# Quarter products of two SwiGLU layers start in another order

## Chip, core and metric

One NeuronCore of a Trainium2 chip runs the whole program. The metric is the device time of one execution in microseconds (us). The kernel before has a median of 958.43 us over three runs (958.37, 958.43 and 960.74). One other execution was profiled, and all rows shown here come from it.

## What is computed

A streaming-encoder block on `x` of shape (1, 512, 1024), all in float32. Cut to the parts that matter here:

```python
h = h + 0.5 * _swiglu(_rmsnorm(h, ffn1_norm[i]), ffn1_w_in[i], ffn1_w_out[i])   # first layer
z = _rmsnorm(h, mix_norm[i]) @ w_in[i]          # convolution module and gated linear attention
h = h + concat([y_conv, y_gla]) @ w_out[i]
h = h + 0.5 * _swiglu(_rmsnorm(h, ffn2_norm[i]), ffn2_w_in[i], ffn2_w_out[i])   # second layer
gate = sigmoid(_rmsnorm(h, ple_norm[i]) @ ple_w_gate[i])
h = h + gate * (p[i] @ ple_w_proj[i])           # then a last rmsnorm

def _swiglu(x, w_in, w_out):
    gate, up = split(x @ w_in, 2)
    return (silu(gate) * up) @ w_out
```

Each of the two SwiGLU layers has 1024 inputs, 2816 gate and 2816 up columns, and 512 tokens. They are the two "layers" of this text.

## The kernel before, in words

**Three products for one.** Every float32 operand is split into a high part (rounded to float32r) and a low part (what is left), and each product is three matmuls: high x high, high x low, low x high. ScalarE (ACT) casts the high part of a weight (`wh`), VectorE (DVE) subtracts to get the low part (`wl`); this is `part` (L406). In the other way, `add_part` (L412, through `added`, L198), ACT writes the negated weight into `wl`, and a DMA that GpSimd (POOL) issues adds the weight to it, so that DVE has no work.

**Seven products for eight.** The 2816 gate columns go in 11 pairs of 128-column blocks, numbered 0 to 10. A pair's weight has four quarters: `a11`, `a12` for the gate (rows 0 to 511 and 512 to 1023 of the input), `a21`, `a22` for up. The tokens are two halves. A pair is done as 2x2 blocks in the manner of Strassen and Winograd, with seven products of 24 matmuls each (128x256), named m1 to m7: m1 uses `a11`, m2 `a12`, m4 `a22`; m6, m7, m5 and m3 use the weight sums `s2`, `s3`, `s1`, `s4` that DVE makes (`s12`, `s3_`, `s4_`, L417 to L434). On the other side stand `b` quarters and their sums `t1` to `t4` (class `Right`, L329), which ACT and DVE split as well (`split`, L360). Below, m1(2) is product m1 of pair 2.

**Banks.** m1 opens the PSUM bank `p.x`; ACT copies it to `p.a` (`sq` in the profile). m6 adds to the same bank; ACT copies that to `p.u2` (`u` in the profile), and m5, which adds to the bank once more, has to wait for that copy (L673 to L683). m2 has its own bank `p.y`. m7 opens `p.w`; DVE reads it in m5's `plus` (`u<-ps,sq`), and m4, which adds to `p.w`, has to wait for that (L681 to L687).

**The gates.** After m2, `gate0` (L668) adds m1's copy to m2's bank and multiplies by the row scale on DVE (two instructions, `g`), and ACT takes silu of it (`s`). It was put behind the next product's preparations.

**The order.** `ffn` (L604) lists *units*, a product each, and `drive` (L584) writes them out: ahead of each product come the preparations that are due for later ones, `AHEAD` = 4 units early for a split on DVE, 6 units for `add_part`, 7 and 9 for a fetch, 6 for sums. The engines run their instructions strictly in that order. In the first layer pair 1 runs as a plain product without sums (units h0 to h7, 128x512) while the token sums are prepared; then pairs 2 to 10 follow. In the second layer pair 1 is the first in quarters. Between the products stand pieces of the second matmul (`w_out`, `wo` below), two 12-matmul groups of 128x512 at a time. Weights come by DMAs that SyncE (SP) issues, into six raw buffers (`wr`); an issue waits until its buffer is free.

The starting order is written out by hand: m1(start), m2(start), m1(start+1), and then for each pair m6, m7, m5, the next pair's m2, m4, m3 (L826 to L844). Pair 2 of the first layer is the first in quarters, so start = 2 there, and start = 1 in the second.

Of the kernel before, what the change touches and what calls it, by code (L numbers as in the profile page):

```python
# [62 lines left out]
def block_kernel(ctx: ExitStack, tc: tile.TileContext, a: dict, out: bass.AP):  # L63
# [29 lines left out]
    def tmp(s, w=SEQ, dt=F32, bufs=2):  # L93
        return tp.tile([P, w], dt, tag=s, bufs=bufs, name=nm(s))

    def bank():
        return pp.tile([P, SEQ], F32, tag="mm", bufs=7, name=nm("ps"))

    def aux():
        return pp.tile([P, SEQ], F32, tag="aux", bufs=1, name=nm("ax"))  # L100
# [113 lines left out]
    def ahead(src, c0, ncol):  # L214


        return [[added(w) for w in high4(load(src, 0, DC, c, P))] for c in range(c0, c0 + ncol, P)]
# [41 lines left out]
    def spread(col, copy=True):  # L259

        ps = aux()
        for j in range(TB):
            pe.transpose(ps[:, j * P:(j + 1) * P], col[:, j:j + 1].to_broadcast([P, P]), ident)
        if not copy:
            return ps
        bc = tmp("bc", bufs=1)
        act.copy(bc, ps)
        return bc
# [17 lines left out]
    class Norm:  # L286
# [5 lines left out]
        def add(self, h):  # L292
            if self.n == 0:
                act.activation(self.acc, h, AF.Square)
            else:
                sq = tmp("sq", bufs=3)
                act.activation(sq, h, AF.Square)
                self.engine.tensor_tensor(out=self.acc, in0=self.acc, in1=sq, op=ALU.add)
            self.n += 1
# [8 lines left out]
    def mul(ps, w, x, first, last, ks=range(4)):  # L308

        (wh, wl), k0 = w, ks[0]  # L310
        for k in ks:
            xh, xl = x[k]
            for i in range(2):
                cs = slice(i * P, (i + 1) * P)
                o = ps[:, i * HALF:(i + 1) * HALF]
                end = last and k == ks[-1] and i == 1
                pe.matmul(o, wh[:, k - k0, cs], xh, start=(first and k == ks[0] and i == 0), stop=False, skip_group_check=True)
                pe.matmul(o, wh[:, k - k0, cs], xl, start=False, stop=False, skip_group_check=True)
                pe.matmul(o, wl[:, k - k0, cs], xh, start=False, stop=end, skip_group_check=True)
# [117 lines left out]
    ffn1_in = a["ffn1_w_in"][0]  # L437
    hT = [big.tile([P, SEQ], F32, tag="H", bufs=DC, name=nm("h")) for _ in range(DC)]
    hg, xps, xt, squares = [], [], {}, []
# [74 lines left out]
    w1 = Left(ffn1_in, 2)  # L514
# [9 lines left out]
    ps0 = [bank() for _ in range(4)]  # L524
    split_w(0, 1, dve.tensor_copy)
    split_x(0)
    mid = []
# [22 lines left out]
    xb = Right(hg, "ffn1_norm")  # L550
    steps = xb.steps()
# [49 lines left out]
        for f in left:  # L601
            f()

    def ffn(w_in, w_out, x, gname, given, first, rsb, hooks, plain, adds=()):  # L604


        norm = Norm()
        nhg = []
        got = {}
        npair = DFF // (2 * P)  # L610
        start = 1 + len(plain)
        end = npair - 1
        pairs = {i: given.get(i) or Left(w_in, 2 * i) for i in range(npair)}

# [8 lines left out]
        def silu(g):  # L623
            s = tmp("s")
            act.activation(s, g, AF.Silu)
            return s

        def plus(ps, t, i, name):
            o = tmp(name)
            dve.tensor_tensor(out=o, in0=ps, in1=t, op=ALU.add)  # L630
            dve.tensor_tensor(out=two(o), in0=two(o), in1=row(i), op=ALU.mult)
            return o
# [11 lines left out]
        def snap(ps, name, **kw):  # L644
            o = tmp(name, **kw)
            act.copy(o, ps)
            return o
# [16 lines left out]
        def m2(p):  # L664
            p.y = bank()
            mul(p.y, p.part("a12"), x.op["b21"], True, True)

            def gate0():  # L668
                p.s0 = silu(plus(p.y, p.a, 0, "g1"))

            return [gate0]

        def m6(p):  # L673
            mul(p.x, p.part("s2"), x.op["t2"], False, False)
            p.u2 = snap(p.x, "u2", bufs=1)

        def m7(p):
            p.w = bank()
            mul(p.w, p.part("s3"), x.op["t3"], True, False)
# [14 lines left out]
        def plain_unit(j):  # L694

            up, i, k = j // 4, j // 2 % 2, j % 2
            def run(p):
# [17 lines left out]
            return run  # L715

        USES = {"m1": ("a11", m1), "m2": ("a12", m2), "m6": ("s2", m6), "m7": ("s3", m7), "m5": ("s1", m5),
                "m4": ("a22", m4), "m3": ("s4", m3)}

        def unit(kind, i):  # L720
            p = pairs[i]

            def go(run):
                left = run(p)
                hooks.get((kind, i), lambda *_: None)()
                return left

            if kind[0] == "h":
                j = int(kind[1])
                part, run = (f"a{1 + j // 4}{1 + j % 2}", plain_unit(j)) if j % 4 < 2 else (None, plain_unit(j))  # L730
                if part:
                    make = p.add_part if (kind, i) in adds else p.part
                    return [(AHEAD, lambda: make(part)), (9, lambda: p.fetch(part))], lambda: go(run)
            else:
                part, run = USES[kind]
            if (kind, i) in adds:
                before = [(AHEAD + 2, lambda: p.add_part(part))]
            else:
                before = [(AHEAD + (kind == 'm5'), lambda: p.part(part))] if part else []
            if kind in ("m1", "m2"):  # L740
                before.append((7, lambda: p.fetch(part)))
            elif kind == "m6":
                before += [(9, lambda: p.fetch("a21", "a22")), (6, p.s12)]
            elif kind in ("m7", "m3"):
                before.append((6, p.s3_ if kind == "m7" else p.s4_))

            return before, lambda: go(run)
# [63 lines left out]
        def add(kind, i):  # L811
            if 0 <= i < npair and (kind, i) not in had:
                had.add((kind, i))
                units.append(unit(kind, i))
# [3 lines left out]
        for i in plain:  # L818
# [4 lines left out]
                    due = due[1:]  # L823
            if i in cut_of:
                due += second(cut_of[i])
        add("m1", start)  # L826
        add("m2", start)
        add("m1", start + 1)
        for i in range(start, npair):
            add("m6", i)  # L830
            add("m7", i)
# [34 lines left out]
    w_in = a["w_in"][0]  # L866
    w_ahead = []

    def sums_hooks(x, names, at):

        h = {}
        for name, key in zip(names, at):
            h[key] = lambda *_, name=name: x.split(name)
        return h

    hooks = sums_hooks(xb, ("t2", "t3", "t1", "t4"), (("h2", 1), ("h3", 1), ("h4", 1), ("m1", 2)))
    hooks.update({("h0", 1): lambda *_: [f() for f in steps[2:4]], ("h1", 1): steps[4]})
    hooks.update({("m5", 3): lambda *_: made[0](), ("m5", 4): lambda *_: constants(),
                  ("m4", 10): lambda *_: w_ahead.append(ahead(w_in, D_CONV, 2 * P)),
                  ("last", 4): lambda *_: w_ahead.append(ahead(w_in, 0, 2 * P))})  # L880
    hg, norm = ffn(ffn1_in, a["ffn1_w_out"][0], xb, "mix_norm", {0: Left(ffn1_in, 0), 1: w1},
                   (ps0[:2], ps0[2:]), lambda: spread(mid[0]), hooks, (1,),
                   {("h4", 1), ("m1", 2), ("m2", 2), ("m4", 2)})
    pool.on = False
    cw, gwu, mean, mask, nbias = made

# [61 lines left out]
    mid = []  # L948
# [10 lines left out]
    rs, rsb = mid  # L959
# [16 lines left out]
    for k0 in range(0, DC, 4):  # L976
        for i in range(2):
            for j in range(4):
                pe.matmul(ps[2 * RANK * j:2 * RANK * (j + 1)], gw[:, k0 + j, :], hg[k0 + j][i].bitcast(F32),
                          start=(k0 == i == 0), stop=(k0 + i == 5), skip_group_check=True)  # L980
# [337 lines left out]
    ffn2_in = a["ffn2_w_in"][0]  # L1318
    wf = {i: Left(ffn2_in, 2 * i) for i in range(3)}
    w0, w1 = wf[0], wf[1]  # L1320
# [40 lines left out]
    norm = Norm()  # L1361
# [57 lines left out]
    hg = nhg  # L1419

    def plain_block(p, up, i, mid={}):
        ps = bank()
        cs = slice(i * P, (i + 1) * P)
        for k in range(DC):
            if k in mid:
                mid[k]()
            wh, wl = p.part(f"a{1 + up}{1 + k // 4}")
            mm3(ps, wh[:, k % 4, cs], wl[:, k % 4, cs], *hg[k], k == 0, k == DC - 1)
        return ps

    mid = []
    xb = Right(hg, "ffn2_norm")
    steps = xb.steps()
# [4 lines left out]
    g0 = plain_block(w0, 0, 0)  # L1438
    steps[1]()
    steps[2]()  # L1440
    u0 = plain_block(w0, 1, 0, {4: lambda: mid.append(norm.rows())})
# [4 lines left out]
    g1_ = plain_block(w0, 0, 1, {1: lambda: mid.append(spread(mid[0]))})  # L1446
# [5 lines left out]
    u1_ = plain_block(w0, 1, 1)  # L1452
    xb.split("t1")
    w1.part("s3")
    hooks = sums_hooks(xb, ("t4",), (("m2", 1),))
# [63 lines left out]
    def todo(*fs):  # L1519
        return lambda *_: [f(*v) for f, *v in fs]  # L1520
# [4 lines left out]
                  ("rest", 2): todo((q_high, b21, q21, 0), (first_sum, 0), (third_sum, 0)),  # L1525
                  ("rest", 4): todo((q_high, b21, q21, 1), (first_sum, 1), (third_sum, 1)),
                  ("rest", 6): todo((final_in,), (row_sums, 0))})
    hg, norm = ffn(ffn2_in, a["ffn2_w_out"][0], xb, "ple_norm", wf, ((g0, u0), (g1_, u1_)), mid[1], hooks, ())

# [143 lines left out]
    def kept(ps, name, **kw):  # L1675
        o = tmp(name, **kw)
        act.copy(o, ps)
        return o
# [20 lines left out]
    t1, t3 = q11, q12  # L1699
    n2_ = [x for jp in range(2) for x in split_rows(n2, jp)]  # L1700
    project(0)
    m1 = [kept(p_, "sq", bufs=3) for p_ in x_]
# [98 lines left out]
```

## Time and profile before

| | us |
|---|---|
| Median of three runs | 958.43 |
| Profiled execution, its own time | 958.56 |
| Its span in the profile | 956.8 |
| TensorE (PE) busy | 936.5 (98%) |
| DVE busy | 762.8 (80%) |
| ACT busy | 484.9 (51%) |

The profile's rows read: start, duration, engine, line, operation, output <- inputs, and in brackets the idle time before it and what ended that. Nearly all instructions have line 46, a recorder's, so that they are told apart by their tiles.

### The profile page before, as it was taken

What the parts mean: (1) busy time and instruction counts of PE and PEld (TensorE: products, weight loads), DVE (VectorE), ACT (ScalarE), POOL (GpSimd) and SP (SyncE); (2) the same over time, 40 slices, a digit from 0 to 9 for tenths busy, and PEclk for the clock granted to TensorE, in tenths of its full rate; (3) what the DMA queues carried; (4) which work ended last, traced back from release to release, by engine and by line L of the source; (5) the groups of instructions that cost most, each with busy time, mean ns of one, the idle gap of its engine ahead of it and who ended that gap; (6) DMA issues with size and microseconds to landing.
All of it is one profiled execution on the core that took longest, in us unless ns stands there. A gap on an engine that the chain in (4) does not pass through costs nothing.

```text
span 956.8 us, 14725 instructions
## 1 busy us (share of the span) xinstructions
PE 936.5 (98%) x5914; PEld 835.7 (87%) x5914; DVE 762.8 (80%) x1037; ACT 484.9 (51%) x729; POOL 57.7 (6%) x75
## 2 busy tenths in 40 slices
PE   9997999999999999999999999999999999999996
PEld 7887999999999988788877889999999999998885
DVE  5787778877878666999987689887887787875896
ACT  5863434344444463374564775444334443445882
POOL 0100010000000020101020010000000000000131
PEclk9998999999999999999999999999999999999999
DMA  7644233423243395337454563323343224347463
GB/s 227 178 111 132 80 100 108 125 79 106 89 132 94 94 245 144 89 66 199 94 117 121 133 133 109 111 84 104 100 132 90 88 88 133 95 133 231 94 110 110
DMA packets 108264, 115.01 MB, mean 120 GB/s; under 512 B 5203, under 2 KB 96517, under 8 KB 108196
## 3 DMA queue, kind: packets, MB, share of 16 engines
q1 hardware_dynamic: 101732, 94.67, 32.1%
q0 software_dynamic: 6448, 19.40, 11.2%
q8 instruction: 46, 0.75, 0.3%
q14 instruction: 22, 0.18, 0.1%
q10 hardware_dynamic: 16, 0.00, 0.0%
HBM read 93.61 MB, written 2.10 MB: 100 GB/s over the span
## 4 chain that ended last, share of the span: by engine, by line
PE 92%; DVE 4%; ACT 3%; issue 1%; POOLq 0%; POOL 0%; ACTq 0%; DVEq 0%
PE ps L46 90%; PE ax L46 1%; ACT wh L46 1%; DVE wl L46 1%; DVE g L46 1%; ACT xg L46 1%; ACT s L46 0%; ACT wl L46 0%; DVE m L46 0%; ACT sq L46 0%; DVE sm L46 0%; DVE xg L46 0%; DVE t1L L46 0%; DVE u L46 0%; DVE wr L46 0%
## 5 line engine op out<-in xcount | busy, mean ns | idle before, releaser
L46 PE MATMUL ps<-hgH,wl 128*128 128x256 f32 (+1 forms) x768 | 230.9, 306 | 2.0 <-DVE wl L46 1.9
L46 PE MATMUL ps<-hgH,wh 128*128 128x256 f32 (+1 forms) x768 | 232.5, 308 | 0.0
L46 PE MATMUL ps<-hgL,wh 128*128 128x256 f32 (+1 forms) x768 | 230.9, 306 | 0.0
L46 DVE TENSOR_TENSOR wl<-wr,wh 128x1024 fp32r<-128x1024 f32 (+2 forms) x160 | 187.5, 1182 | 47.5 <-ACT wh L46 47.4
L46 ACT CAST wh<-wr 128x1024 fp32r<-128x1024 f32 (+2 forms) x178 | 179.3, 1021 | 18.7 <-issue 6.7
L46 PEld LDWEIGHTS ps<-hgH,wl 128*128 128x128 f32 x768 | 146.8, 191 | 9.2 <-DVE wl L46 2.5
L46 PEld LDWEIGHTS ps<-hgH,wh 128*128 128x128 f32 x768 | 147.1, 192 | 8.6 <-issue 1.1
L46 PEld LDWEIGHTS ps<-hgL,wh 128*128 128x128 f32 x768 | 146.4, 191 | 6.8 <-issue 0.2
L46 PE MATMUL ps<-actH,wh 128*128 128x512 f32 x352 | 137.5, 391 | 0.0
L46 PE MATMUL ps<-actL,wh 128*128 128x512 f32 x352 | 137.4, 390 | 0.0
L46 PE MATMUL ps<-actH,wl 128*128 128x512 f32 x352 | 136.9, 389 | 0.0
L46 ACT ACTIVATE s<-g 128x512 f32<-128x512 f32 x48 | 30.4, 634 | 200.6 <-DVE g L46 200.6
L46 DVE SCALAR_TENSOR_TENSOR cv<-glu,cw,cv 128x502 f32<-128x502 f32 (+24 forms) x120 | 81.1, 733 | 0.6
L46 PEld LDWEIGHTS ps<-actH,wl 128*128 128x128 f32 x352 | 66.1, 188 | 14.0
L46 PEld LDWEIGHTS ps<-actH,wh 128*128 128x128 f32 x352 | 66.2, 188 | 12.8
L46 PEld LDWEIGHTS ps<-actL,wh 128*128 128x128 f32 x352 | 66.2, 188 | 12.4
L46 DVE SCALAR_TENSOR_TENSOR h<-ps,h 128x512 f32<-128x512 f32 x80 | 54.2, 687 | 19.2 <-PE ps L46 19.2
L46 ACT COPY sq<-ps 128x512 f32<-128x512 f32 x42 | 24.5, 585 | 78.7 <-PE ps L46 78.7
L46 DVE TENSOR_TENSOR wl<-sm,wh 128x1024 fp32r<-128x1024 f32 x42 | 51.0, 1222 | 3.3 <-ACT wh L46 3.1
L46 PE MATMUL ps<-t1H,wh 128*128 128x256 f32 x152 | 44.4, 292 | 8.0 <-ACT u L46 8.0
L46 ACT CAST wh<-sm 128x1024 fp32r<-128x1024 f32 x42 | 43.9, 1046 | 6.0 <-DVE sm L46 3.3
L46 PE MATMUL ps<-t1L,wh 128*128 128x256 f32 x152 | 44.1, 290 | 0.0
(267 smaller groups left out, 1774.6 us busy)
## 6 DMA issues: line engine op xcount, KB each, us to landing
wr<-in_ffn_w_in SPq DMA_DIRECT2D x84, 512.0 KB
wr<-in_ffn_w_out SPq DMA_DIRECT2D x32, 512.0 KB
wr<-in_w_in SPq DMA_DIRECT2D x20, 512.0 KB
wl<-wr POOLq DMA_DIRECT2D x19, 512.0 KB, 5.1
wr<-in_ffn_w_out SPq DMA_DIRECT2D x16, 384.0 KB
wr<-in_w_out SPq DMA_DIRECT2D x8, 512.0 KB
wq<-in_ple_w_gate SPq DMA_DIRECT2D x8, 512.0 KB
wl<-wq POOLq DMA_DIRECT2D x8, 512.0 KB, 4.9
```

What stands on the lines that cost most here:

```text
L46: inst = call(*args, **kwargs)
```

## The change

It does three things.

1. Both layers get a number `lead`. The gate of the pair `start + lead - 1` isn't left behind the next product; it is held and written out in m6 of pair `start`, right behind the copy of u2. In the first layer `lead` is 2, so that this is the gate of pair 3; in the second it is 1, the gate of pair 1.
2. In the first layer the plain products of two pairs come first: m1(2), m2(2), m1(3), m2(3), and then m6(2). m2(3) moves from behind m5(2) to ahead of m6(2).
3. In the first layer the weight sums of pair 2 are made in h3 and h4, with the splits of `t3` and `t1`, and the set of products whose low parts are added by DMA changes: m1(2) leaves it (DVE subtracts again), m1(3) and m2(3) join it.

```diff
-    def ffn(w_in, w_out, x, gname, given, first, rsb, hooks, plain, adds=()):
+    def ffn(w_in, w_out, x, gname, given, first, rsb, hooks, plain, lead, adds=()):
...
+        held = []
...
                 p.s0 = silu(plus(p.y, p.a, 0, "g1"))
+            if p is pairs[start + lead - 1]:
+                held.append(gate0)
+                return []
             return [gate0]
         def m6(p):
             mul(p.x, p.part("s2"), x.op["t2"], False, False)
             p.u2 = snap(p.x, "u2", bufs=1)
+            for f in held:
+                f()
+            held.clear()
...
-        add("m1", start)
-        add("m2", start)
-        add("m1", start + 1)
+        for i in range(start, start + lead):
+            add("m1", i)
+            add("m2", i)
+        if lead == 1:
+            add("m1", start + 1)
...
+    wf = {i: Left(ffn1_in, 2 * i) for i in (2,)}
+    hooks.update({("h0", 1): lambda *_: [f() for f in steps[2:4]], ("h1", 1): steps[4],
+                  ("h3", 1): lambda *_: [xb.split("t3"), wf[2].s12()], ("h4", 1): lambda *_: [xb.split("t1"), wf[2].s3_()]})
...
-                   {("h4", 1), ("m1", 2), ("m2", 2), ("m4", 2)})
+                   (ps0[:2], ps0[2:]), lambda: spread(mid[0]), hooks, (1,), 2,
+                   {("h4", 1), ("m2", 2), ("m4", 2), ("m1", 3), ("m2", 3)})
...
-    hg, norm = ffn(ffn2_in, a["ffn2_w_out"][0], xb, "ple_norm", wf, ((g0, u0), (g1_, u1_)), mid[1], hooks, ())
+    hg, norm = ffn(ffn2_in, a["ffn2_w_out"][0], xb, "ple_norm", wf, ((g0, u0), (g1_, u1_)), mid[1], hooks, (), 1)
```

**First place: ACT ahead of m1(2), first layer.** Before, where `wr_495` is `a11` of pair 2, `wr_520` its `a12`, and `s` the silu of plain gates:

```order
L46 CAST wh_497<-wr_429 128x1024
L46 CAST wh_522<-wr_495 128x1024
L46 ACTIVATE wl_523<-wr_495 128x1024
L46 ACTIVATE s_529<-g_117_527 128x512
L46 CAST t2H_544<-xg_422 128x512
L46 CAST t2H_548<-xg_491 128x512
L46 CAST wh_554<-wr_520 128x1024
L46 ACTIVATE wl_555<-wr_520 128x1024
L46 CAST t3H_571<-xg_416 128x512
L46 CAST t3H_575<-xg_482 128x512
L46 ACTIVATE s_581<-g_131_579 128x512
```

And now, where `wr_495` is still `a11` of pair 2, `wr_516` its `a12`, and `wr_547` is `a11` of pair 3:

```order
L46 CAST wh_497<-wr_429 128x1024
L46 ACTIVATE s_520<-g_113_518 128x512
L46 CAST t2H_535<-xg_422 128x512
L46 CAST t2H_539<-xg_491 128x512
L46 CAST wh_549<-wr_516 128x1024
L46 ACTIVATE wl_550<-wr_516 128x1024
L46 CAST t3H_566<-xg_416 128x512
L46 CAST t3H_570<-xg_482 128x512
L46 CAST wh_580<-wr_547 128x1024
L46 ACTIVATE wl_581<-wr_547 128x1024
L46 CAST wh_585<-wr_495 128x1024
L46 ACTIVATE s_591<-g_136_589 128x512
```

The cast of `a11` of pair 2, which the first product in quarters needs, has moved from the second place to the eleventh, behind both a silu and two other weights.

**Second place: DVE between the first weights of pair 3 and m4(2), first layer.** Before, where `sm_844` is the first weight sum of pair 3 (`wr_741` is its `a21`, `wr_743` its `a22`) and `u_181` is the instruction that m4(2) waits for:

```order
L46 TENSOR_TENSOR sm_844<-wr_741,wr_743 128x1024
L46 TENSOR_TENSOR sm_845<-sm_844,wr_552 128x1024
L46 TENSOR_TENSOR wl_849<-wr_520,wh_848 128x1024
L46 TENSOR_TENSOR u_181_878<-ps_819,sq_876 128x512
L46 TENSOR_TENSOR u_181_878<-u_181_878,bc_454 128x512
L46 TENSOR_TENSOR wr_741<-wr_552,wr_741 128x1024
L46 TENSOR_TENSOR wl_883<-wr_786,wh_882 128x1024
```

And now, where these are `sm_850`, `wr_746`, `wr_748` and `u_186`:

```order
L46 TENSOR_TENSOR sm_850<-wr_746,wr_748 128x1024
L46 TENSOR_TENSOR sm_851<-sm_850,wr_547 128x1024
L46 TENSOR_TENSOR wl_855<-wr_516,wh_854 128x1024
L46 TENSOR_TENSOR wr_746<-wr_547,wr_746 128x1024
L46 TENSOR_TENSOR wl_885<-wr_787,wh_884 128x1024
L46 TENSOR_TENSOR u_186_914<-ps_858,sq_912 128x512
L46 TENSOR_TENSOR u_186_914<-u_186_914,bc_454 128x512
```

Two more 1024-wide subtractions now stand ahead of the instruction that m4(2) waits for.

**Third place: DVE where the second layer's gate is held.** Before, where `g_984` is the gate of pair 1, `sm_5711` the first sum of pair 2, and `u_998` is what m4(1) waits for:

```order
L46 TENSOR_TENSOR g_984_5679<-ps_5641,sq_5631 128x512
L46 TENSOR_TENSOR g_984_5679<-g_984_5679,bc_5491 128x512
L46 TENSOR_TENSOR sm_5711<-wr_5598,wr_5600 128x1024
L46 TENSOR_TENSOR sm_5712<-sm_5711,wr_5373 128x1024
L46 TENSOR_TENSOR wr_5598<-wr_5373,wr_5598 128x1024
L46 TENSOR_TENSOR wl_5743<-wr_5034,wh_5742 128x1024
L46 TENSOR_TENSOR wl_5774<-sm_5712,wh_5773 128x1024
L46 TENSOR_TENSOR u_998_5803<-ps_5746,sq_5801 128x512
```

And now:

```order
L46 TENSOR_TENSOR sm_5707<-wr_5599,wr_5601 128x1024
L46 TENSOR_TENSOR sm_5708<-sm_5707,wr_5374 128x1024
L46 TENSOR_TENSOR g_989_5737<-ps_5642,sq_5632 128x512
L46 TENSOR_TENSOR g_989_5737<-g_989_5737,bc_5492 128x512
L46 TENSOR_TENSOR wr_5599<-wr_5374,wr_5599 128x1024
L46 TENSOR_TENSOR wl_5744<-wr_5035,wh_5743 128x1024
L46 TENSOR_TENSOR wl_5775<-sm_5708,wh_5774 128x1024
L46 TENSOR_TENSOR u_998_5804<-ps_5747,sq_5802 128x512
```

The gate's two instructions have moved behind the two sums; the count ahead of `u_998` is the same. On ACT the silu of that gate has moved from ahead of the copies `sq` and `u` to behind them, and still stands ahead of the cast that `wl_5744` needs:

```order
L46 CAST wh_5676<-wr_5376 128x1024
L46 COPY sq_5705<-ps_5680 128x512
L46 COPY u_988_5735<-ps_5607 128x512
L46 ACTIVATE s_5740<-g_989_5737 128x512
L46 CAST wh_5743<-wr_5035 128x1024
L46 CAST wh_5774<-sm_5708 128x1024
```

More of the change, by code (lines that the diff above doesn't have):

```diff
@@ L876, in block_kernel @@
     hooks = sums_hooks(xb, ("t2", "t3", "t1", "t4"), (("h2", 1), ("h3", 1), ("h4", 1), ("m1", 2)))
-    hooks.update({("h0", 1): lambda *_: [f() for f in steps[2:4]], ("h1", 1): steps[4]})
+    wf = {i: Left(ffn1_in, 2 * i) for i in (2,)}
+    hooks.update({("h0", 1): lambda *_: [f() for f in steps[2:4]], ("h1", 1): steps[4],
+                  ("h3", 1): lambda *_: [xb.split("t3"), wf[2].s12()], ("h4", 1): lambda *_: [xb.split("t1"), wf[2].s3_()]})
     hooks.update({("m5", 3): lambda *_: made[0](), ("m5", 4): lambda *_: constants(),
@@ L880, in block_kernel @@
                   ("last", 4): lambda *_: w_ahead.append(ahead(w_in, 0, 2 * P))})
-    hg, norm = ffn(ffn1_in, a["ffn1_w_out"][0], xb, "mix_norm", {0: Left(ffn1_in, 0), 1: w1},
-                   (ps0[:2], ps0[2:]), lambda: spread(mid[0]), hooks, (1,),
-                   {("h4", 1), ("m1", 2), ("m2", 2), ("m4", 2)})
+    hg, norm = ffn(ffn1_in, a["ffn1_w_out"][0], xb, "mix_norm", {0: Left(ffn1_in, 0), 1: w1, 2: wf[2]},
+                   (ps0[:2], ps0[2:]), lambda: spread(mid[0]), hooks, (1,), 2,
+                   {("h4", 1), ("m2", 2), ("m4", 2), ("m1", 3), ("m2", 3)})
     pool.on = False
```

## The prediction

> **What bounds the kernel now.** I read the page's chain first: TensorE has nearly all of it.
>
> ```profile
> PE 92%; DVE 4%; ACT 3%; issue 1%; POOLq 0%; POOL 0%; ACTq 0%; DVEq 0%
> ```
>
> So only what stops PE counts. The waits of PE (total, times, longest) name two that the change can touch:
>
> ```profile
> PE ps L46 <- ACT u L46: 8.0, 2, 6.1
> PE ps L46 <- DVE wl L46: 1.9, 2, 1.7
> ```
>
> The wait for `u` is m5's for the copy of u2, once in each layer. PE's timeline shows the long one, in the first layer:
>
> ```profile
> 65.88 0.28 PE L46 MATMUL ps<-t2H,wh 128*128 128x256 f32 x1
> 68.76 0.28 PE L46 MATMUL ps<-t3H,wh 128*128 128x256 f32 x1
> 71.52 0.28 PE L46 MATMUL ps<-t3H,wl 128*128 128x256 f32 x1
> 77.86 0.58 PE L46 MATMUL ps<-t1H,wh 128*128 128x256 f32 x1 [6.06 <-ACT u L46]
> 83.15 0.31 PE L46 MATMUL ps<-hgH,wh 128*128 128x256 f32 x1
> 86.06 0.40 PE L46 MATMUL ps<-actH,wh 128*128 128x512 f32 x1
> 91.52 0.28 PE L46 MATMUL ps<-hgH,wh 128*128 128x256 f32 x1
> ```
>
> m6(2) begins at 65.88 and m7(2) at 68.76: a product costs 2.88 us. m5(2) begins 6.2 us late, at 77.86, and takes 5.29 us instead of 2.88. m2(3) follows, then two `wo` groups of 5.46 us together, and m4(2) at 91.52. The windows tell why m5 is slow (the columns after DVE's are ACT's, POOL's, the granted clock, the DMA share and GB/s):
>
> ```profile
> 71.80:77.80 6.00, 0.00 (x1) 0.00 (x0) 4.10 (x5) 3.38 (x6) 0.86 (x1) 0.88 0.47 90
> 77.80:83.20 5.40, 5.34 (x25) 5.34 (x26) 3.70 (x4) 0.96 (x2) 0.00 (x0) 0.50 0.62 192
> ```
>
> The clock was at 0.50 after the stop: 2.41 us more. The stop costs 8.6 us in all, and there is 1.7 us ahead of it and 1.9 us in the second layer. That is the most that can go, some 12 us.
>
> **The change, first layer, step by step.** I add durations along each engine's queue in the new order, on the clock of this profile. Up to 49 us nothing differs. ACT before:
>
> ```profile
> 44.85 2.00 ACT L46 CAST wh<-wr 128x1024 fp32r<-128x1024 f32 x2
> 49.90 0.63 ACT L46 ACTIVATE s<-g 128x512 f32<-128x512 f32 x1 [2.10 <-DVE g L46]
> 52.43 1.06 ACT L46 ACTIVATE wl<-wr 128x1024 fp32r<-128x1024 f32 x1
> 53.38 1.13 ACT L46 CAST t3H<-xg 128x512 fp32r<-128x512 f32 x2
> ```
>
> A 1024-wide cast takes 0.95 us from start to start, a 512-wide one 0.52. The second of the casts at 44.85 is `a11` of pair 2. Now that cast stands behind the silu at 49.90, which still waits for DVE, and behind two more weights. ACT reaches it after the `t3` casts, at 53.38 + 1.04 + 1.90 = 56.3, and ends it at 57.4. Its low part is DVE's:
>
> ```profile
> 55.05 0.28 PE L46 MATMUL ps<-hgH,wh 128*128 128x256 f32 x1
> 54.03 1.30 DVE L46 TENSOR_TENSOR t3L<-xg,t3H 128x512 fp32r<-128x512 f32 x2 [1.65 <-ACT t3H L46]
> 58.34 1.22 DVE L46 TENSOR_TENSOR sm<-wr,wr 128x1024 f32<-128x1024 f32 x1
> 59.60 1.23 DVE L46 TENSOR_TENSOR sm<-sm,wr 128x1024 f32<-128x1024 f32 x1
> 64.34 2.36 DVE L46 TENSOR_TENSOR wl<-sm,wh 128x1024 fp32r<-128x1024 f32 x2
> ```
>
> After the `t3` splits DVE makes the two sums (1.26 + 1.14) and then this `wl`, which ends at 58.9. m1(2) could begin at 55.05; its third matmul, due at 55.29, now comes at 58.97. **A new stop of 3.7 us** takes the place of the 1.7 us one at m1(3), whose low part now comes by DMA. That gate of DVE is late too, so ACT's silu runs at 59.6, and `a12` of pair 3 leaves ACT at 63.2. How long the DMA takes after POOL's issue:
>
> ```profile
> 47.18 0.37 SPq L176 DMA_DIRECT2D wr<-in_ffn_w_in  x1
> 48.11 0.86 POOL L46 DMA_DIRECT2D wl<-wr  x1 [10.80 <-ACT wl L46]
> wl<-wr POOLq DMA_DIRECT2D x1, 512.0 KB, 6.1
> 53.78 0.86 POOL L46 DMA_DIRECT2D wl<-wr  x1 [4.80 <-ACT wl L46]
> wl<-wr POOLq DMA_DIRECT2D x1, 512.0 KB, 4.5
> ```
>
> The one issued at 48.11, beside a load of SP, landed after 6.1 us; the one at 53.78, alone, after 4.5. The new one is issued at 63.5, within 0.2 us of a `w_out` load that goes when the third sum has freed its buffer (63.2). I take 6.1: it lands at 69.6, and m2(3) stops 2.0 us (4.5 would stop it 0.45). PE's list is then m1(2) to 61.6, m2(2) 64.5, m1(3) 67.4, m2(3) 72.2, m6(2) 75.1, m7(2) 78.0.
>
> Is u2 copied in time? On ACT two subtractions' worth of casts for m5 and m7, `a22`, the silu of gate 2, a copy and a `wo` cast lie ahead; DVE's gate ends at 73.1 and the copy begins when m6 has ended, about 75.2. **So m5's stop goes**, and with it the half clock: m5(2) ends at 80.9, the two `wo` groups at 86.3.
>
> **Then m4(2) waits, which it didn't before.** It needs DVE's `u<-ps,sq`, which has two more subtractions ahead. The head of that queue is the first sum of pair 3, and what it waits for is a chain of transfers:
>
> ```profile
> 72.02 0.86 POOL L46 DMA_DIRECT2D wl<-wr  x1 [17.38 <-ACT wl L46]
> 76.62 0.37 SPq L176 DMA_DIRECT2D wr<-in_ffn_w_in  x1
> 80.25 1.23 DVE L46 TENSOR_TENSOR sm<-wr,wr 128x1024 f32<-128x1024 f32 x1 [1.67 <-DMA wr<-in_ffn_w_in]
> 84.00 0.69 DVE L46 TENSOR_TENSOR u<-ps,sq 128x512 f32<-128x512 f32 x1
> ```
>
> `a22` of pair 2 is added by DMA (72.02 to 76.6); that frees a raw buffer, and SP loads `a22` of pair 3 into it (76.62 to 80.2). In the new order ACT hands `a22` over at 71.5, behind the casts for m5 and m7, and POOL issues at 71.8. SP's load of `a21` for pair 3, which was issued at 67.86 before, now goes at 71.9, when m7's `wl` has freed its buffer. So the two run together: 71.8 + 6.1 = 77.9, the load 3.6 more, 81.5. Then 1.26 + 4 x 1.14 for two sums, s4's low part, the third sum and a `wo` low part: 87.3, and 0.7 for `u`. m4(2) begins at 88.05 instead of 91.52. From there on both lists are alike and m2(3) lies behind both, so **the first layer gains 3.5 us**. PE's own new stops (3.7 and 2.0) cost nothing more: without them m4(2) would only wait longer. If POOL's DMA takes 4.5 there, m4(2) begins at 86.5: 5.0 us. DVE comes out of this some 4 us behind PE; the next stop would be m4(3), two thirds of a pair later, and DVE has idle time there (2.45 us ahead of `u`):
>
> ```profile
> 112.19 0.69 DVE L46 TENSOR_TENSOR u<-ps,sq 128x512 f32<-128x512 f32 x1 [2.45 <-ACT sq L46]
> ```
>
> **The change, second layer.**
>
> ```profile
> 586.11 0.38 PE L46 MATMUL ps<-t1H,wh 128*128 128x256 f32 x1 [1.90 <-ACT u L46]
> 584.47 0.63 ACT L46 ACTIVATE s<-g 128x512 f32<-128x512 f32 x1 [3.79 <-DVE g L46]
> 585.47 0.59 ACT L46 COPY u<-ps 128x512 f32<-128x512 f32 x1
> 582.97 0.68 DVE L46 TENSOR_TENSOR g<-ps,sq 128x512 f32<-128x512 f32 x1
> 590.10 0.68 DVE L46 TENSOR_TENSOR u<-ps,sq 128x512 f32<-128x512 f32 x1
> 591.96 0.28 PE L46 MATMUL ps<-hgH,wh 128*128 128x256 f32 x1
> ```
>
> The copy of u2 stood behind a silu that waited for DVE. It now goes at 581.4, when m6 has ended, and m5(1) begins at 584.05, 2.06 us earlier. But m4(1) (at 591.96 now) needs `u` on DVE, ready at 590.8. The gate moves behind two sums, so its silu runs at 586.8 on ACT and the s4 cast behind it ends at 588.4; DVE waits 0.6 us for that, does two `wl` and reaches `u` at 590.7. m4(1) begins at 591.5: **0.4 us gained of 2.06**, and a stop of 1.7 us at m4(1) takes the rest. Clock: the stops of 1.65 and 1.90 us left it at 1.00, so I price these at their length alone. Added by DMA instead of DVE, one product more: one ACT pass and one POOL issue more, 1.2 us of DVE less, all inside the lists above.
>
> **Sum.** 3.5 + 0.4 = 3.9 us off 958.56 gives 954.7; the median of before is 0.13 lower, so I predict **954.6 us**.
>
> **Two rules of the Trainium skill.** The Trainium skill, "TensorE: Matmul & The Clock Gate", Part 1, says that the clock halves after an idle window of about 3.4 us. The trace agrees so far: 6.06 us halved it, 1.90 didn't. By it m1(2)'s stop, with two matmuls inside, may halve the clock; the 2.4 us would end in the waits of m2(3) and m4(2), so the sum stays. The Trainium skill, "DMA: Bandwidth & Descriptors", Queues, rings and completion order, says that each ring takes descriptors in order. By it the load at 77.9 isn't slowed by the `w_out` load issued 0.4 us behind it, and stays at 3.6; no run here shows two such loads.
>
> **Rivals.**
> - *The transfers don't disturb each other* (4.5): m4(2) at 86.5, 5.4 us gained, 953.1. For it: issues only 0.1 us apart, where the 6.1 had a head start of 0.9. Chance 0.2.
> - *The load shares its time with the `w_out` load behind it*: half its 2.9 us of moving more, 1.45, straight onto m4(2): 956.1. Chance 0.16.
> - *A stop at m4(2) reaches the length that halves the clock*: if m2(3)'s DMA is quick and `a22`'s slow, the wait is 3.3 us, and m4(2) takes 2.4 more: 957.0. The clock at 0.50 after 6.06 speaks for it, the 1.00 after 1.90 against. Chance 0.1.
> - *Slower*: the chain from POOL's `a22` DMA to `u` is one to one with the end. It decides when the two transfers take over 13.6 us instead of 9.7; at 15 us the time is 960.0. No transfer of this size in the rows took over 6.1. Chance 0.06.
> - *u2 stays late*, the gate of pair 2 on ACT being no earlier than before: m5(2) would have to stop 4 us again. DVE's gate ends at 73.1 against 75.2 before. 957.5, chance 0.03.
>
> **Chances.** The forecast has 0.45. A measurement of this kernel can tell about 0.3% (2.9 us) from no change. Faster by more than that hold the forecast, mostly (it is 1 us from the edge), and the first rival: 0.64. Within it: 0.29. Slower: 0.07. The range 952.8 to 957.2 holds all but the slower case, the last and the outer edges.
>
> **What would show it.** In the changed profile: no wait for `u` at m5 in either layer and the clock at 1.00 near 80 us; a wait for `wh` and `wl` at m1(2) of 3.5 us near 55; one for the DMA at m2(3); a wait of DVE's `u` at m4 in both layers, 1 to 3 us each. A DVE `u` that is early at m4(2), or a long wait after 110 us, would prove it wrong.

## The result, and the profile after

The changed kernel has a median of 956.85 us over 13 runs (954.73 to 957.53), against 958.48 us for the kernel before in the same comparison (13 runs, 958.11 to 960.74). The ratio, of the means 956.38 and 959.10, is 0.9972, 95% interval 0.9963 to 0.9981. So it is faster, by 1.6 us between the medians and 2.7 between the means. These differ because the runs of both kernels lie in two groups some 2 us apart, and the median of before falls in its lower group, that of the changed kernel in its upper one. The forecast was 954.6 us, a gain of 3.9, with a range from 952.8 to 957.2.

The profiled execution took 957.42 us, with a span of 955.7. The page's chain looks as before:

```profile
PE 90%; issue 4%; DVE 3%; DMA 1%; ACT 1%; POOL 1%; POOLq 0%; DVEq 0%; ACTq 0%; SPq 0%
```

DMA is new in it. The waits of PE (total, times, longest) have changed their names:

```profile
PE ps L46 <- DVE u L46: 4.0, 2, 2.5
PE ps L46 <- ACT wh L46: 2.2, 1, 2.2
PE ps L46 <- DVE wl L46: 1.2, 2, 1.0
PE ps L46 <- DMA wl<-wr: 0.3, 1, 0.3
```

The wait for ACT's `u`, 8.0 us before, is gone in both layers. In its place stand DVE's `u` (the waits of m4) and the new stops at m1(2) and m2(3). PE's timeline in the first layer:

```profile
57.44 0.38 PE L46 MATMUL ps<-hgH,wh 128*128 128x256 f32 x1 [2.19 <-ACT wh L46]
...
58.94 0.39 PE L46 MATMUL ps<-hgH,wl 128*128 128x256 f32 x1 [1.00 <-DVE wl L46]
...
69.67 0.39 PE L46 MATMUL ps<-hgH,wl 128*128 128x256 f32 x1 [0.34 <-DMA wl<-wr]
...
78.17 0.28 PE L46 MATMUL ps<-t1H,wh 128*128 128x256 f32 x1
...
89.22 0.39 PE L46 MATMUL ps<-hgH,wh 128*128 128x256 f32 x1 [2.54 <-DVE u L46]
...
96.54 0.40 PE L46 MATMUL ps<-actH,wh 128*128 128x512 f32 x1
```

m1(2) stops for 2.19 and 1.00 us, m2(3) for 0.34, m5(2) at 78.17 not at all, and m4(2) at 89.22 for 2.54. The last row is the first `wo` matmul behind m4(2) and m3(2); it stood at 97.28 before. From m4(2) to it are 7.32 us, 5.76 before (91.52 to 97.28). The windows tell why (behind the colon the length, then the busy time of PE, PEld, DVE, ACT and POOL, the granted clock, the DMA share and GB/s):

```profile
59.00:59.50 0.50, 0.50 (x4) 0.50 (x5) 0.48 (x1) 0.00 (x0) 0.00 (x0) 0.84 0.98 188
62.50:63.00 0.50, 0.50 (x5) 0.50 (x5) 0.50 (x1) 0.50 (x2) 0.00 (x0) 0.74 0.00 0
90.00:90.50 0.50, 0.50 (x5) 0.50 (x4) 0.50 (x1) 0.00 (x0) 0.00 (x0) 0.56 0.88 283
93.00:93.50 0.50, 0.50 (x4) 0.50 (x4) 0.50 (x2) 0.00 (x0) 0.00 (x0) 0.52 0.17 45
```

The clock was at 0.50 twice: a mean of 0.84 in the first of these half microseconds means that it fell at 59.34, one of 0.74 that it rose at 62.76. In the same way the second spell lies from 90.06 to 93.48.

What released m4(2) shows in the chain of waits in order of time:

```profile
71.66 6.95 DMA wl<-wr
...
78.66 3.92 DMA wr<-in_ffn_w_in
...
82.67 1.24 DVE sm L46
...
85.08 1.22 DVE wl L46
86.30 1.13 DVE wr L46
87.43 1.14 DVE wl L46
...
88.56 0.61 DVE u L46
...
89.22 21.58 PE ps L46 x144
```

This is the chain of the forecast: the adding DMA of `a22` of pair 2, the load of `a22` of pair 3 into the buffer that it frees, the sums, `u`, m4(2).

In the second layer PE stops once, at m4(1):

```profile
580.64 0.59 ACT L46 COPY u<-ps 128x512 f32<-128x512 f32 x1 [0.23 <-PE ps L46]
586.12 0.63 ACT L46 ACTIVATE s<-g 128x512 f32<-128x512 f32 x1 [4.89 <-DVE g L46]
587.72 1.23 DVE L46 TENSOR_TENSOR wl<-wr,wh 128x1024 fp32r<-128x1024 f32 x1 [0.56 <-ACT wh L46]
590.74 0.39 PE L46 MATMUL ps<-hgH,wh 128*128 128x256 f32 x1 [1.50 <-DVE u L46]
```

The copy comes as soon as m6 has ended, the silu stands behind it, and the cast behind the silu holds DVE for 0.56 us.

**A measure by stage.** The executions start unequally: the first silu of the first layer's gates ran at 48.95 to 51.22 us in the profiles shown here. So I compare three stretches, each read from PE's and ACT's timelines: A from that silu (49.90 before) to the first `wo` matmul behind m3(2) (97.28 before); B from there to the first `wo` matmul of pair 3 (117.51); C from there to the first one of the second layer (612.12).

| kernel (label) | first silu | A | B | C | median of runs |
|---|---|---|---|---|---|
| before | 49.90 | 47.38 | 20.23 | 494.61 | 958.48 |
| changed | 49.94 | 46.60 | 20.23 | 494.23 | 956.85 |
| changed (after_again) | 49.60 | 46.57 | 20.23 | 494.32 | 957.15, one run |
| changed (after_again2) | 49.31 | 45.04 | 20.22 | 494.21 | 955.23, one run |
| l2_only | 49.53 | 47.58 | 20.24 | 494.26 | 957.85 |
| hold_only | 49.77 | 41.78 | 20.52 | 494.21 | 953.20 |
| late_sums | 51.08 | 43.05 | 24.88 | 494.24 | 958.05 |
| no_m4_dma | 48.95 | 42.91 | 20.23 | 494.26 | 952.89 |
| no_hold_l1 | 51.21 | 45.23 | 20.24 | 494.20 | 957.10 |
| a11_early | 49.41 | 44.16 | 20.23 | 494.20 | 954.46 |
| hold_late2 | 49.35 | 43.27 | 20.23 | 499.68 | 958.72 |
| best | 50.05 | 39.10 | 21.01 | 498.67 | 954.79 |
| best_l1 | 51.22 | 39.11 | 21.01 | 494.19 | 950.71 |
| best_u | 49.97 | 39.10 | 21.02 | 493.14 | 949.40 |

The first layer gained 0.78 us (A), the second 0.38 (C). A adds up: before, 47.38 less the stops of 1.65 and 6.06 and the 2.41 of half clock is 37.26 of work. After, the stops are 2.19 + 1.00 + 0.34 + 2.54 = 6.07, and 46.60 - 37.26 - 6.07 leaves 3.27 for the two spells of half clock, of which 1.56 is m4(2)'s. The stops shrank by 1.64 us, and the half clock grew by 0.86.

### The profile page after: what moved, and what is told of

Read it like the earlier page. It is cut to its first block, busy times and chain, and to the rows that moved or that the text cites. A ratio compares the mean times of both kernels' runs of the same rounds, so it can differ in the third digit from the quotient of the medians.

```text
span 955.7 us, 14720 instructions
## 1 busy us (share of the span) xinstructions
PE 937.4 (98%) x5914; PEld 836.1 (87%) x5914; DVE 761.2 (80%) x1036; ACT 484.6 (51%) x730; POOL 58.4 (6%) x76
## 4 chain that ended last, share of the span: by engine, by line
PE 90%; issue 4%; DVE 3%; DMA 1%; ACT 1%; POOL 1%; POOLq 0%; DVEq 0%; ACTq 0%; SPq 0%
PE ps L46 88%; PE ax L46 1%; DVE wl L46 1%; DMA wl<-wr 1%; DMA wr<-in_ffn_w_in 0%; DVE sm L46 0%; POOL wl L46 0%; DVE g L46 0%; ACT wh L46 0%; POOL rs L46 0%; ACT s L46 0%; DVE u L46 0%; DVE wr L46 0%; DVE y L46 0%; DVE ssx L46 0%
## 5 line engine op out<-in xcount | busy, mean ns | idle before, releaser
L46 PE MATMUL ps<-t2H,wl 128*128 128x256 f32 x152 | 43.0, 283 | 0.0
```

What stands on the lines that cost most here:

```text
L46: inst = call(*args, **kwargs)
```

## The experiments

The theory was that m4(2) is set by the chain of transfers, and that the half clock behind its stop takes the rest. The rivals were that DVE simply has too much work, that PE's new stop at m1(2) sets the end, and that the new order is what gives the gain. Medians of before in the three comparisons were 958.36, 958.62 and 958.50 us. Diffs are against the changed kernel, unless another is named.

**Second layer alone.** The first layer as before, no gate held there:

```diff
+            if lead and p is pairs[start + lead - 1]:
...
-                   (ps0[:2], ps0[2:]), lambda: spread(mid[0]), hooks, (1,), 2,
-                   {("h4", 1), ("m2", 2), ("m4", 2), ("m1", 3), ("m2", 3)})
+                   (ps0[:2], ps0[2:]), lambda: spread(mid[0]), hooks, (1,), 0,
+                   {("h4", 1), ("m1", 2), ("m2", 2), ("m4", 2)})
```

> Only the second layer has the held gate; the first layer is that of the kernel before. If the gain of the second layer is cut short by the next wait: m5(1) has no stop, m4(1) stops 1.5 us for DVE's u, and the span is 0.4 us under before's 956.8. If the copy of u2 was all that the second layer waited for: m4(1) has no stop either and the span is 1.9 to 2.1 us under. The long stop of 6 us at m5(2) of the first layer and the half clock behind it stay.

957.85 us, ratio 0.9990 (0.9981 to 0.9998). C is 0.35 us shorter, and m4(1) stops 1.51 us. The step of the second layer holds; its rival, that the 1.9 us come free, falls.

**The hold alone, in both layers.** The diff is the same with `lead` 1 in the first layer too.

> The gate is held in both layers (lead is 1 in both), but the order of the products, the weight sums and the set added by DMA are those of before. If the silu ahead of the copy was all that held m5(2): the copy of u2 ends near 73.8 instead of 77.8, m5(2) stops 2.2 us instead of 6.06 and starts near 73.9; without the old wait m4(2) starts at 85 to 86.7 instead of 91.5, and the time is 951.7 to 953.3, below that of the changed kernel. That the new order and the sooner sums are needed (the rival) would show in a stop at m4(2) of 3 us or more, or a stop at m5(2) that stays over 4 us, and a time of 956 or more.

953.20 us, ratio 0.9945 (0.9933 to 0.9957): **one part of the change alone gives 5.2 us by the medians, the whole 1.6**. PE's and SP's rows in the first layer:

```profile
74.47 0.39 PE L46 MATMUL ps<-t1H,wh 128*128 128x256 f32 x1 [2.81 <-ACT u L46]
67.72 9.12 SPq L176 DMA_DIRECT2D wr<-in_ffn_w_in  x2
```

m5(2) stops 2.81 us, a little more than expected, and m4(2) not at all. SP's first load of this pair, `a21` of pair 3, goes at 67.72, in the changed kernel only at 71.75. So the adding DMA runs without it. The rows of the adding DMAs (last number: us from issue to landing) are, for `a22` here, for `a22` in the changed kernel, and for m2(3)'s weight there:

```profile
wl<-wr POOLq DMA_DIRECT2D x1, 512.0 KB, 4.5
```

```profile
wl<-wr POOLq DMA_DIRECT2D x1, 512.0 KB, 7.0
...
wl<-wr POOLq DMA_DIRECT2D x1, 512.0 KB, 6.2
```

The rival of this run, that the order and the sooner sums are needed, falls.

**The sums of pair 3 behind `u` on DVE.** The transfers stay.

```diff
+            elif kind == "m6" and i == start + 1 and i in (3,):
+                before = [(9, lambda: p.fetch("a21", "a22")), (4, p.s12)] + before
+            elif kind == "m7" and i == start + 1 and i in (3,):
+                before = [(4, p.s3_)] + before
```

> The changed kernel with the sums s1, s2 and s3 of pair 3 written behind m5(2)'s u on DVE; the transfers are as they were. If m4(2) is late because DVE takes its instructions in order and the sums that stand ahead of u wait for a transfer: the stop of 2.5 us at m4(2) and the half clock behind it (1.6 us) go, m4(2) starts at 86.7 instead of 89.2, and the time is 4.2 us under the 957.4 of the changed kernel's profiled run, 953.2. If DVE simply has too much work, or if PE's stop of 3.2 us at m1(2) sets the end: within 1 us of the changed kernel.

958.05 us, ratio 0.9991 (0.9982 to 0.9999): a miss. Four rows tell why; this execution, of 959.68 us, was the slowest of the 12:

```profile
85.32 1.05 ACT L46 CAST wh<-wr 128x1024 fp32r<-128x1024 f32 x1 [4.80 <-DMA wr<-in_ffn_w_out]
86.40 1.23 DVE L46 TENSOR_TENSOR wl<-wr,wh 128x1024 fp32r<-128x1024 f32 x1 [4.62 <-ACT wh L46]
88.28 0.39 PE L46 MATMUL ps<-hgH,wh 128*128 128x256 f32 x1 [0.69 <-DVE u L46]
108.41 0.39 PE L46 MATMUL ps<-t1H,wh 128*128 128x256 f32 x1 [2.90 <-ACT u L46]
```

The stop at m4(2) did shrink from 2.54 to 0.69 us, and m4(2) starts 2.1 us earlier, counted from the first silu (37.20 us behind it instead of 39.28; 2.5 were expected). A is 3.55 shorter, some 3 of it because this execution had no half clock in A at all, not even behind m1(2), which stopped as long as before (2.18 and 0.99 us). The stop didn't vanish, because the chain has a second arm that I had not seen: SP issues the `w_out` load behind that of `a22`. ACT's cast of it, at 85.32, stands ahead of the `sq` that `u` reads, and DVE's subtraction of the same weight, at 86.40, waits for the cast and stands ahead of `u` itself, which starts at 87.55. And the sums are now late for pair 3: m5(3) stops 2.90 us for its copy of u2, with a half clock behind it, so that B is 4.65 longer. The work put behind `u` has no free place there; DVE's place in line is the cause at m4(2), but its amount is that of the next stop.

**`a22` of pair 2 without the adding DMA.**

```diff
-                   {("h4", 1), ("m2", 2), ("m4", 2), ("m1", 3), ("m2", 3)})
+                   {("h4", 1), ("m2", 2), ("m1", 3), ("m2", 3)})
```

> The changed kernel, but the low part of a22 of pair 2 is DVE's subtraction and not a DMA that adds. If the chain DMA of a22, load of a22 of pair 3, sums, u sets m4(2): the raw buffer is free some 6 us sooner, the load starts near 72 instead of 78.7, the sums near 77 to 78 instead of 82.7, m4(2) has no stop or one under 1 us, and the time is near 953.2. If it is DVE's work that makes u late: one subtraction more ahead of u, m4(2) 1.1 us later, time 958.5.

952.89 us, ratio 0.9941 (0.9929 to 0.9953), as the theory has it; the rival had 958.5. SP's two loads and the first sum:

```profile
70.75 5.04 SPq L176 DMA_DIRECT2D wr<-in_ffn_w_in  x2
79.12 1.22 DVE L46 TENSOR_TENSOR sm<-wr,wr 128x1024 f32<-128x1024 f32 x1 [1.27 <-DMA wr<-in_ffn_w_in]
```

The second load goes at 70.75 + 5.04 - 0.37 = 75.4. That is 26.5 us behind the first silu instead of 28.7, so 2.2 us sooner; I had expected 6.7, but the buffer waits for DVE's subtraction now. `u` starts 2.6 us sooner by the same count (84.93 here, 88.48 in the changed kernel). The stop at m4(2) is gone, and the half clock behind it; the one at m1(2) is still there. A is 3.69 shorter than in the changed kernel with one more subtraction on DVE. That the transfers made `u` late is shown; that there is too much work on DVE falls for this stop.

**The new order without the hold in the first layer.**

```diff
-            if p is pairs[start + lead - 1]:
+            if not plain and p is pairs[start + lead - 1]:
```

> The changed kernel, but in the first layer no gate is held: pair 3's stands ahead of the copy of u2 of pair 2 again, in the new order of products. If m4(2) is set by the chain of transfers, the hold is worth nothing here: the copy of u2 ends about 2.5 us later, m5(2) stops 2 to 2.5 us, that stop comes out of the one at m4(2), which then is under 0.5 us, and the time is within 1 us of the changed kernel, or up to 1.6 us less, where the half clock behind the stop at m4(2) goes with it. If the hold carries the gain of the first layer: m4(2) starts 2 us later or more and the time is 959 or more.

957.10 us, ratio 0.9973 (0.9961 to 0.9985), the same as the changed kernel. PE's two rows:

```profile
80.24 0.39 PE L46 MATMUL ps<-t1H,wh 128*128 128x256 f32 x1 [0.52 <-ACT u L46]
90.59 0.38 PE L46 MATMUL ps<-hgH,wh 128*128 128x256 f32 x1 [1.74 <-DVE u L46]
```

The hold was worth 0.52 us at m5(2) (2 to 2.5 expected), and m4(2)'s wait gives that back: m4(2) starts 39.38 us behind the first silu, against 39.28. That A is 1.37 us shorter in this execution is the half clock behind m4(2), which a stop of 1.74 us did not bring. In the new order pair 2's gate is through before m6(2) has ended, and pair 3's delays the copy by little. So there the hold gains nothing, and the reordering did the hold's work at a higher price.

**`a11` of pair 2 by DMA again.**

```diff
-                   {("h4", 1), ("m2", 2), ("m4", 2), ("m1", 3), ("m2", 3)})
+                   {("h4", 1), ("m1", 2), ("m2", 2), ("m4", 2), ("m1", 3), ("m2", 3)})
```

> The changed kernel with the low part of a11 of pair 2 added by DMA again, so that m1(2) finds its weight in time; the stop of 3.2 us there and the half clock behind it go. If the chain of transfers sets m4(2): PE comes to m4(2) earlier and waits longer there, and the time stays within 1 us of the changed kernel. If PE's stop at m1(2) sets the end (the rival): 3 to 5 us less, 952.5 to 954.5.

954.46 us, ratio 0.9948 (0.9935 to 0.9960): by its number this stands with the rival, by its rows not.

```profile
67.90 0.58 PE L46 MATMUL ps<-hgH,wl 128*128 128x256 f32 x1 [3.99 <-DMA wl<-wr]
69.99 0.86 POOL L46 DMA_DIRECT2D wl<-wr  x1 [7.41 <-ACT wl L46]
87.71 0.39 PE L46 MATMUL ps<-hgH,wh 128*128 128x256 f32 x1 [1.46 <-DVE u L46]
```

m1(2) no longer stops, but m2(3) stops 3.99 us for its DMA, so PE gains little ahead of m4(2), which still waits. What came out is the chain: POOL issues `a22` at 69.99, 20.58 us behind the first silu instead of 21.72. The 1.14 us are the subtraction of `a11` that DVE no longer makes. m4(2) starts 0.98 us earlier by the same count (38.30 against 39.28), and from m4(2) to the `wo` matmul PE takes 5.86 us instead of 7.32, as the clock stays at 1.00 behind a stop of 1.46; together that is the 2.44 by which A is shorter. The stop at m1(2) cost nothing; the subtraction behind it did.

**The hold alone, and the second layer's sums and weights of pair 2 behind `u`.** This comes on top of the diff of the hold alone.

```diff
+            elif kind == "m6" and i == 2 and not plain:
+                before = [(9, lambda: p.fetch("a21", "a22")), (3, p.s12), (3, lambda: p.part(part))]
+            elif kind == "m7" and i == 2 and not plain:
+                before = [(3, p.s3_), (3, lambda: p.part(part))]
+            elif kind == "m5" and i == 2 and not plain:
+                before = [(4, lambda: p.part(part))]
```

> The kernel with only the hold, in both layers, and in the second layer the sums and weights of pair 2 behind the u that m4(1) waits for, on DVE. If DVE's place in line alone makes u late there: m4(1) has no stop, nothing later takes its place, and the time is 1.5 us under that of the hold alone (953.2), 951.7. If the late sums make m6(2), m7(2) or m5(2) of the second layer wait, as the same step did in the first layer: no gain, 953.2 or more.

958.72 us, ratio 0.9992 (0.9983 to 1.0001): the second case. m4(1) has no stop, but m5(2) of this layer has one of 4.36 us. C is 5.45 longer than in the changed kernel: 4.36 less the 1.50 saved at m4(1), and the rest for a spell of half clock from 600.29 to 607.12.

```profile
601.22 0.58 PE L46 MATMUL ps<-t1H,wh 128*128 128x256 f32 x1 [4.36 <-ACT u L46]
```

**The last kernel, with another set of DMAs in the first layer.**

```diff
-                   {("h4", 1), ("m1", 2), ("m2", 2), ("m4", 2)})
+                   {("h4", 1), ("m1", 2), ("m2", 2), ("m1", 3)})
```

> As the kernel before this one, and in the first layer the low part of a11 of pair 3 is added by DMA, and that of a22 of pair 2 is DVE's subtraction. The stop of 1.66 us at m1(3) goes, the copy of u2 comes about 0.9 us sooner since ACT has one pass less ahead of it, and the raw buffer of a22 is free sooner: 2 to 2.6 us less, about 949.4. If DVE has no room for a subtraction more ahead of u (the rival), m4(2) stops 1 us or more and the gain is under 1.5 us.

954.79 us, ratio 0.9948 (0.9934 to 0.9961). The 949.4 missed because its base did; against that base it is 3.9 us less, where 2 to 2.6 were expected. By the profiles A is 4.17 us shorter, and about 1.5 of that is the half clock that the base's execution had behind m5(2) of the first layer and this one hasn't. In the first layer only stops of 0.57 and 1.19 us are left, and A is 39.10.

**The two parts that worked, together.** The diff of the hold alone and that of the last kernel; the second layer is that of the changed kernel:

> Hold only, in both layers, with a11 of pair 3 added by DMA and a22 of pair 2 subtracted by DVE; the second layer as in the changed kernel. The first layer of this set has shown stops of 0.6 and 1.2 us only; the second layer gives back the 5.5 us that the late sums cost there. 949.3, and no less than 948.5. If the first layer's gain came from what the late sums did elsewhere, it is 952 or more.

950.71 us, ratio 0.9919 (0.9907 to 0.9932). The expected time was 1.4 lower, the rival's 952 or more; B is 0.8 longer than in the changed kernel, with a stop of 0.53 at m5(3).

**One weight alone behind `u` in the second layer**, against the kernel above.

```diff
+            elif kind == "m6" and i == 2 and not plain:
+                before = [(9, lambda: p.fetch("a21", "a22")), (6, p.s12), (3, lambda: p.part(part))]
```

> As the kernel before this one, and in the second layer one instruction alone, the low part of s2 of pair 2, behind the u that m4(1) waits for. The stop of 1.5 us at m4(1) shrinks by the 1.14 us of that instruction to 0.4 us, DVE's work behind it stays in time (m6(2) is due 5.8 us after m4(1)), and the time is 1.1 us less, 948.2. If any delay of pair 2's weights costs as the late sums did: m5(2) of the second layer stops for its copy, and the time is 949.5 or more.

949.40 us, ratio 0.9905 (0.9890 to 0.9920), the fastest of all, 9.1 us under before. C is 1.05 shorter than in the kernel above, and m5(2) of the second layer doesn't stop, so the rival falls. PE's waits, and m4(1):

```profile
PE ps L46 <- ACT u L46: 1.7, 2, 1.2
...
PE ps L46 <- DVE u L46: 0.4, 1, 0.4
```

```profile
582.97 0.39 PE L46 MATMUL ps<-hgH,wh 128*128 128x256 f32 x1 [0.37 <-DVE u L46]
```

**The changed kernel, profiled twice more.**

> The changed kernel once more, for another profiled execution. Its executions lie in two groups, near 955.2 and near 957.3. If the groups come from the half clock behind the stop at m4(2) (and from the start of the program, which differs by up to 2 us between the profiles so far): an execution of the lower group shows the same stop of about 2.5 us at m4(2) with the clock at 1.00 behind it, or an earlier start; one of the upper group shows the half clock. If the groups come from the transfers: an execution of the lower group shows a DMA of a22 that lands in under 6 us and a stop at m4(2) of under 1.5 us.

> As the run before this one, a third profiled execution of the changed kernel, with the same expectations: in the lower group the clock stays at 1.00 behind m4(2)'s stop or the program starts sooner, with the stop itself unchanged; the rival has the stop shorter and the DMA of a22 quicker.

The first took 957.15 us and shows the half clock behind a stop of 2.61 us at m4(2). The second took 955.23; m4(2)'s row and a window behind it:

```profile
88.50 0.39 PE L46 MATMUL ps<-hgH,wh 128*128 128x256 f32 x1 [1.89 <-DVE u L46]
```

```profile
89.00:90.00 1.00, 1.00 (x10) 1.00 (x10) 1.00 (x2) 0.00 (x0) 0.00 (x0) 1.00 1.01 313
```

The clock stayed at 1.00. m4(2) starts 39.19 us behind the first silu, against 39.28: the transfers are no quicker. The stop is shorter only because the half clock at m1(2) lasted longer and PE came later. Of the 1.9 us between the two runs 1.53 lie in A and 0.29 in the start. Both executions had 6.8 us of half clock in all. In the first one 3.4 us of it lay at m1(2) and 3.4 behind m4(2); in the second all of it lay at m1(2) (57.59 to 64.42), where the wait at m4(2) takes it up. So in the executions profiled, two of the upper group and one of the lower, the place of the half clock parts the groups; what makes the start differ was not tried.

## Why the prediction was right and the gain too large

- **m1(2)'s new stop**: its third matmul was forecast at 58.97 and came at 58.94. That the stop itself costs nothing holds. The sum also had the late silu behind its DVE subtraction (59.6, measured 59.52). What the text doesn't say is that this subtraction thereby stands at the head of the chain to m4(2) and costs 1.14 us there.
- **m2(3)**: the DMA took 6.2 us (6.1 taken), and the third matmul came at 69.67. The stop was 0.34 and not 2.0, because m1(2)'s half clock had made PE late, as the text allowed.
- **u2 in time**: m5(2) at 78.17, without a stop (78.0 forecast).
- **m4(2) late through the transfers**: the mechanism was right in each of its links. Two terms were too small. "I take 6.1" for the DMA of `a22` measured 6.95, and the load behind it 3.92 instead of 3.6. Together they make m4(2) start at 89.22 instead of 88.05. The 6.1 was one row; DMAs with the same neighbour took 6.0 to 6.9 us in the other profiles. The 3.6 of the row before was kept on the argument, drawn from the order within a ring, that the `w_out` load behind it doesn't slow it. That load was issued 0.47 us behind (79.13), and the 3.92 doesn't bear the argument out, though the second rival's 1.45 us more was too much.
- **The clock**: this is the step that failed. The prediction read the clock as a matter of the stop's length, "6.06 halved it, 1.90 didn't", and gave m4(2)'s stop a chance of 0.1 to halve it. A stop of 2.54 us halved it, for 1.56 us; it is the place of a stop, not its length alone, that decides (last section). So the third rival came true, with a stop shorter than its 3.3 us and a price below its 2.4. 3.5 forecast, less 1.17 and 1.56, is 0.77; A shows 0.78.
- **The second layer**: 0.4 forecast, 0.38 measured, and the stop at m4(1) 1.50 (1.7 forecast).
- **Behind m4(2)**: B is the same to 0.01 us in the changed kernel and before; no later stop took its place, as forecast.
- **Luck**: the median lies 0.35 us inside the range, and five of the 13 runs lie above it. Seven runs fall in the upper group (956.85 to 957.53), near the third rival's 957.0, and six in the lower (954.73 to 955.84), near the forecast, so the median could as well have come out 1 us lower. The gain is under 2.9 us by medians and by means: that is the case that was given 0.29, not the one given 0.64.

The Trainium skill, "TensorE: Matmul & The Clock Gate", Part 1, says that the window of about 3.4 us runs freely, so that the moment of the transition depends on where in it the first matmul lands. The runs agree: the clock's falls and rises lie on one grid of 3.41 us in each trace, and the prediction used only the window's length. They also show that a window need not be idle throughout: 1.97 to 2.82 us of idle time in one was followed by half the clock too.

## What to carry to other kernels

When a stop is taken away, follow the next consumer of the same queue back to its transfers: here the gain depended on a buffer that a DMA had to free. Try the parts of a change singly: the hold alone brought 5.2 us, and the reordering around it took most of that back, by moving a load next to an adding DMA and a subtraction ahead of its source. An instruction may be put behind a late one only where the engine has idle time before its own consumer: one subtraction behind `u` gained 1.05 us, four operations lost 5.5. A stop of PE between 2 and 3.4 us is best priced twice, with a halved clock behind it and without.

## What the runs showed of the hardware

**The same stop may or may not halve the clock.** Two kernels with the same first layer up to there, hold_only and hold_late2, stopped 2.81 and 2.82 us at m5(2). PE's row of the second, and one window of it, then the same moment of the first:

```profile
74.06 0.39 PE L46 MATMUL ps<-t1H,wh 128*128 128x256 f32 x1 [2.82 <-ACT u L46]
```

```profile
75.00:76.00 1.00, 1.00 (x7) 1.00 (x6) 1.00 (x2) 0.00 (x0) 0.00 (x0) 0.50 0.36 66
```

```profile
75.00:76.00 1.00, 1.00 (x10) 1.00 (x10) 1.00 (x2) 0.00 (x0) 0.00 (x0) 1.00 0.83 156
```

The one ran at 0.50, the other (hold_only, 74.47) at 1.00. A is 1.49 us longer for it (43.27 against 41.78). The spells were 3.42 us in the changed kernel, twice; before, the clock fell at 76.4, in the stop itself, and rose at 83.2, 6.8 us or twice as long.

The times of the changes show what lies behind this. In the changed kernel they are 59.34, 62.76, 90.06 and 93.48 us, which is 1, 8 and 1 times 3.41 us apart. The next one, near the program's end, is at 950.22, 251 steps behind, which makes a step 3.4133 us. In each of the 14 traces all changes of the clock lie whole steps of this length apart. So each trace can be cut into such steps. The step with the stop in hold_late2, and then the two in hold_only:

```profile
71.22:74.64 3.42, 0.60 (x6) 0.58 (x6) 2.52 (x3) 2.79 (x4) 0.86 (x1) 1.00 0.59 114
```

```profile
69.27:72.68 3.41, 2.40 (x21) 2.19 (x19) 2.43 (x7) 3.41 (x5) 0.81 (x1) 1.00 0.39 134
72.68:76.10 3.42, 1.63 (x13) 1.63 (x14) 3.42 (x4) 1.74 (x3) 0.05 (x1) 1.00 0.81 153
```

In hold_late2 the clock fell at 74.64. The step before that holds the whole stop: PE was idle for 2.82 of its 3.42 us. In hold_only the clock fell only near the end, at 946.50. A boundary 256 steps ahead of that, at 72.68, cuts the stop in two: 1.01 us of idle time in one step, 1.79 in the next, and the clock stayed.

The same count over all 14 traces, from 48 to 130 and from 570 to 625 us: behind each of the 14 steps with 1.97 us or more of idle time the clock was halved, behind none with 1.79 or less. At the end of the program one step with 1.98 us went without, so the limit lies near 2 us. A halved clock came back behind a step with at most 0.34 us of idle time and stayed behind those with 0.65 to 1.49, which makes spells of one step or two. So where an execution's steps fall decides what a stop of 2 to 3.4 us costs. This is read from the traces; no run set the steps on purpose.

**An adding DMA of 512 KB takes 4.5 to 4.6 us with no load beside it, 6.0 to 6.3 with a `w_out` load issued 0.2 us ahead of it and 6.8 to 7.0 with the load of `a21` issued 0.1 us behind it**, in each profile with these neighbours. With a load of `in_ffn_w_in` issued 0.9 us ahead (the one at 48 us) it took 6.0 to 6.9. The Trainium skill, "DMA: Bandwidth & Descriptors", Issuing engines are not separate DMA queues, has them share the same 16 engines. Why these times differ was not tried, nor were the loads moved apart with all else the same.
